# A two-layer hybrid decoder trunk: six of a layer's nine transposed projection blocks computed by rows, their queries and keys turned by VectorE, and work of GpSimd and VectorE moved to ScalarE

## The chip, the cores and the metric

The kernel runs on one core of one Trainium2 chip. The metric is device microseconds of one execution. Three executions of the kernel before gave 931.69, 933.27 and 933.47 us, a median of 933.27 us. The profiled execution, from which all rows below come, took 931.93 us by itself, with a span of 930.2 us from its first to its last instruction.

## The reference: what is computed

One sequence of 256 tokens goes through two layers of width 2048. A layer is a pre-norm mixer: one wide input projection (7700 columns) feeds four groups of four heads each, every group's output is multiplied by a gate path, and one output projection is added to the residual.

```python
def hybrid_layer(x, layer_idx, norm_g, w_in, ..., w_out, rope_diff, rope_moba):
    h = rms_norm(x, norm_g)
    p = split_columns(jnp.einsum("bsd,de->bse", h, w_in))
    log_f = jax.nn.log_sigmoid(p["fox_f"] + fox_fb)            # fox: softmax with a cumulative forget bias
    fox = forgetting_attention(q, k, v, log_f)                 # logit = q.k/sqrt(d) + F[t] - F[s]
    fox = from_heads(fox) * jax.nn.silu(p["fox_g"])
    q1, q2, k1, k2 = (partial_rope(t, *rope_diff) for t in (q1, q2, k1, k2))
    diff = differential_attention(q1, q2, k1, k2, v, lam)      # softmax(q1 k1) - lam softmax(q2 k2)
    diff = from_heads(rms_norm(diff, diff_norm_g) * (1.0 - lambda_init)) * jax.nn.silu(p["diff_g"])
    mq, mk = partial_rope(moba_q, *rope_moba), partial_rope(moba_k, *rope_moba)
    moba = from_heads(moba_attention(mq, mk, v)) * jax.nn.silu(p["moba_g"])
    gla = gla_chunked(q, k, v, log_a)                          # gated linear attention
    gla = from_heads(rms_norm(gla, gla_norm_g)) * jax.nn.silu(p["gla_g"])
    mixed = jnp.concatenate([fox, diff, moba, gla], axis=-1)
    return x + jnp.einsum("bse,ed->bsd", mixed, w_out)
```

The rotation of `partial_rope` touches a quarter of each head: 16 of 64 elements for diff, 32 of 128 for moba. After the second layer stands one more RMSNorm.

## The kernel before

**Products in three parts.** Weights and activations are 32-bit. Each is split into a high part that TensorE takes in its fp32r form and a low part with the rest; a product is hi·hi + lo·hi + hi·lo. ScalarE makes the high part of the weights (`hi`, line L185 in the trace is the helper that all VectorE and ScalarE calls go through), VectorE subtracts it (`lo<-raw,hi`).

**Steps.** The weights come in 304 steps of about 512 KB, 152 in each layer, in the order of a table made by `_steps` (steps 0 to 151 are layer 0, 152 to 303 layer 1). A step is one slice of one block; a block is a set of output columns (512 mostly) over all 2048 inputs. `load` sends a step's weights from the SP queue into one of 4 `raw` buffers. `parts_of` makes hi and lo in one of 4 `hi` and 4 `lo` buffers. `multiply` issues the matmuls. The Python loop at the end writes the program: in iteration i it first prepares step i+3 (hi and lo), then `settle` hands on the results of finished blocks, then step i is multiplied, then `tick` advances the background tasks (all the attention work, as generators). Every engine runs its instructions strictly in the order in which this loop wrote them, so a task's VectorE operation written in iteration i stands behind the `lo` of step i+3. That `lo` waits for a `hi`, and the `hi` of step i+3 waits until TensorE has read the `hi` of step i-1, which had the same buffer.

**Two kinds of block.** A block of kind "rows" has the activations as the stationary operand and 512 columns of weights moving: 12 matmuls of 512 columns a step (2 of the 16 input tiles, 2 halves of the tokens, 3 parts). A block of kind "cols" comes in two half-blocks of 256 columns, has the weights as the stationary operand, and gives the result transposed: 8 matmuls of 512 columns (both activation parts side by side in `hTp`) and 8 of 256 columns a step of 4 input tiles. A layer has nine such transposed blocks: gla_q with gla_k, fox_q, fox_k, fox_g, diff_q, diff_k, moba_q, moba_k, moba_g. Their result leaves PSUM by `columns` or `rotated`: a ScalarE copy (`both<-mm`), a VectorE addition (`both<-mm,both`), and a VectorE product, per half-block; for diff and moba also a shuffle on VectorE and a product on GpSimd for the rotation.

**PSUM.** Blocks accumulate in two `mm` buffers in turn, so a block can begin when the block before the last has been read out. The tasks' products go to two `side` buffers.

**Results that must wait.** `settle` holds a finished block back while a key that it needs is not ready (for moba_q the rotation table `rope_m`, which the task `turning` loads and scales by the row norms `rb`). When two finished blocks wait at the start of a new one, `settle` advances all tasks without limit (`tick(False)`) until the keys are there. In the same way the loop advances all tasks before a step of the output projection whose group of inputs (`mTh`, `mTl`, four groups) isn't ready yet. Otherwise `tick` stops when VectorE or ScalarE would get more work than TensorE's matmuls leave time for, by the estimates in `Costed`; the tasks that stand later in the list are then not advanced.

**Output projection.** Its blocks take the groups in the order gla, fox, diff, moba; the first two blocks are interleaved so that the moba inputs are asked for late. In the table of before the two blocks run over gla, fox and diff one after the other (6 steps each) and then over moba (2 steps each).

Of the kernel before, what the change touches and what calls it, by code (L numbers as in the profile page):

```python
# [21 lines left out]
P = 128  # L22
# [4 lines left out]
H = 4  # L27
# [11 lines left out]
T4 = 8  # L39
# [23 lines left out]
def _constants():  # L63
# [10 lines left out]
    put("after", (i[:, None] > i[None, :]))  # L74
    put("heads", np.stack([i < 64, i >= 64], 1))
    put("upto", (i[:, None] <= i[None, :]), "b")
# [6 lines left out]
    for name, half, dim in (("rope_d", DIFF_HALF, 64), ("rope_m", MOBA_HALF, HD)):  # L83
# [3 lines left out]
        cos, sin = np.ones((dim, SEQ), np.float32), np.zeros((dim, SEQ), np.float32)  # L87
        cos[:half] = cos[half:rot] = np.cos(ang)
        sin[:half], sin[half:rot] = -np.sin(ang), np.sin(ang)
        put(name, np.tile(np.concatenate([cos, sin], 1), (P // dim, 1)))  # L90
# [4 lines left out]
KEPT = CAT["rope_d"][0]  # L95


def _blocks():
# [37 lines left out]
def _steps():  # L136
# [78 lines left out]
def hybrid_trunk(  # L215
# [8 lines left out]
    diff_norm_g: bass.AP,  # L224
    gla_wa2: bass.AP,
    gla_ba: bass.AP,
    gla_norm_g: bass.AP,
# [59 lines left out]
    def turned(dst, src):  # L287


        for j in range(4):  # L290
            for i in range(4):
                a, b = slice(32 * i, 32 * i + 32), slice(32 * j, 32 * j + 32)
                v_.us += 0.14
                v_.transpose(dst[(b,) + (slice(None),) * (len(dst.shape) - 2) + (a,)],
                             src[(a,) + (slice(None),) * (len(src.shape) - 2) + (b,)])
            yield

# [10 lines left out]
    after = cst("after")  # L308
# [3 lines left out]
    dng = cp.tile([P, DEPTH, HD], F32, name="dng")  # L312
    gng = cp.tile([P, DEPTH, HD], F32, name="gng")
    wa = cp.tile([17, DEPTH, 256], F32, name="wa")
    upto_r = cp.tile([P, P], F32R, name="upto_r")
# [9 lines left out]
    nc.vector.memset(halfpow, -0.5)  # L325
    nc.vector.memset(one, 1.0)

    zeros = s4.get([P, 512], BF16)
    nc.vector.memset(zeros, 0.0)

# [10 lines left out]
    def constants():  # L341
# [5 lines left out]
        s = []  # L347
        for name in ("upto", "masks"):
            c, n = CAT[name]
            s.append(s4.get([P, n], BF16))  # L350
            nc.scalar.dma_start(s[-1], const_b[:, c:c + n])
# [357 lines left out]
    def softmax_part(m, qT, kT, rows, scale, su, forget=None):  # L709
# [3 lines left out]
        for kt in range(m + 1):  # L713
            dst = S[:, kt]
            if forget is not None:
                forget(dst, m, kt)
# [181 lines left out]
    def fox_k(l, ps, half):  # L898
# [4 lines left out]
        if half == 0:  # L903
            return
# [503 lines left out]
```

## Time and profile before

| | us |
|---|---|
| median of three executions | 933.27 |
| the profiled execution | 931.93 |
| its span | 930.2 |
| TensorE busy (matmul) | 918.1 |
| VectorE busy | 739.7 |
| ScalarE busy | 469.7 |
| GpSimd busy | 70.4 |

The span is what the instructions cover; the execution's own time is 1.7 us more. Matmuls are pipelined, so their durations overlap: what one costs in a row of equals is the distance between starts, not its own duration. A timeline row merges equal instructions that follow one another: start, time covered, engine, line, operation, tiles, count; in brackets how long the engine was idle before, and what released it. In the names of tiles buffer numbers are left out: `mm` and `side` are PSUM, `four` and `two` are work buffers of 4 KB and 2 KB per partition.

### The profile page before, as it was taken

The numbers are of one execution on the slowest core, as the hardware profiler recorded it, in microseconds if no ns is written. First come the engines' busy times: TensorE is split into PE (matmuls) and PEld (weight loads), VectorE is DVE, ScalarE is ACT, GpSimd is POOL, SyncE is SP. The second block draws the span as 40 slices with busy tenths as digits, with TensorE's granted clock in tenths as the row PEclk, the third lists the DMA queues.
The fourth block names the chain that finished last, engine by engine and source line by source line (L and its number), as shares of the span: only waits on it lengthen the run. The fifth ranks groups of instructions, "written<-read, shape, count | busy, mean of one in ns | idle before, by whom it ended". The sixth has DMA issues, their size and how long they took to land.

```text
span 930.2 us, 13911 instructions
## 1 busy us (share of the span) xinstructions
PE 918.1 (99%) x5302; PEld 803.1 (86%) x5302; DVE 739.7 (80%) x1181; ACT 469.7 (50%) x646; POOL 70.4 (8%) x45
## 2 busy tenths in 40 slices
PE   9999999999999999999999999999999999999996
PEld 7989889889888798888898898898888888888886
DVE  7668887899769979959856878777985898898663
ACT  7665634453474346444646553456446544463541
POOL 0011201001111100000000302000111101100000
PEclk9999999999999999999999999999999999999998
DMA  8766565555545565565654554554455546656452
GB/s 297 233 196 205 202 187 166 159 180 180 184 161 168 162 223 178 191 178 178 206 175 151 178 181 154 175 182 157 160 181 191 183 153 211 214 193 202 161 180 91
DMA packets 48645, 169.90 MB, mean 183 GB/s; under 512 B 5921, under 2 KB 6465, under 8 KB 48578
## 3 DMA queue, kind: packets, MB, share of 16 engines
q1 hardware_dynamic: 46304, 164.98, 54.4%
q10 hardware_dynamic: 1634, 1.93, 0.8%
q0 software_dynamic: 640, 2.10, 0.8%
q8 instruction: 41, 0.67, 0.3%
q14 instruction: 26, 0.21, 0.1%
HBM read 166.89 MB, written 2.10 MB: 182 GB/s over the span
## 4 chain that ended last, share of the span: by engine, by line
PE 94%; DVE 2%; DMA 1%; issue 1%; ACT 0%; SPq 0%; POOLq 0%; POOL 0%; DVEq 0%; ACTq 0%
PE mm L281 86%; PE side L281 8%; DVE lo L185 1%; DMA four<-in_xt 1%; DMA raw<-in_weights 1%; DVE four L185 0%; DVE tq L185 0%; PE side L285 0%; ACT hi L185 0%; DVE hTp L185 0%; DVE xs L185 0%; SPq L1185 0%; POOLq L1404 0%; POOL rf L392 0%; DVE both L185 0%
## 5 line engine op out<-in xcount | busy, mean ns | idle before, releaser
L185 ACT ACTIVATE hi<-raw 128x1024 fp32r<-128x1024 f32 (+3 forms) x301 | 317.5, 1059 | 402.9 <-PE mm L281 317.2
L185 DVE TENSOR_TENSOR lo<-raw,hi 128x1024 fp32r<-128x1024 f32 (+3 forms) x301 | 381.0, 1274 | 148.4 <-ACT hi L185 145.2
L281 PE MATMUL mm<-hTp,hi 128*128 128x512 f32 x1120 | 274.3, 393 | 0.0
L281 PEld LDWEIGHTS mm<-hTp,hi 128*128 128x128 f32 x1120 | 204.0, 188 | 39.7 <-issue 0.3
L281 PE MATMUL mm<-hi,hTp 128*128 128x512 f32 (+2 forms) x1024 | 196.3, 339 | 0.3 <-ACT hi L185 0.3
L281 PEld LDWEIGHTS mm<-hi,hTp 128*128 128x128 f32 x1024 | 161.0, 189 | 21.9 <-issue 0.7
L281 PEld LDWEIGHTS mm<-hTp,lo 128*128 128x128 f32 x1120 | 144.1, 191 | 5.5
L281 PE MATMUL mm<-hTp,lo 128*128 128x256 f32 x1120 | 147.3, 283 | 0.0
L281 PE MATMUL mm<-lo,hTp 128*128 128x512 f32 (+2 forms) x512 | 105.5, 338 | 0.2
L281 PEld LDWEIGHTS mm<-lo,hTp 128*128 128x128 f32 x512 | 80.9, 188 | 12.1 <-DVE lo L185 2.5
L185 DVE STREAM_TRANSPOSE four<-four 32x256 f32<-32x256 f32 x160 | 69.7, 435 | 2.5
L281 PE MATMUL mm<-hi,mTh 128*128 128x512 f32 (+1 forms) x256 | 64.6, 377 | 0.0
L281 PE MATMUL mm<-lo,mTh 128*128 128x512 f32 (+1 forms) x256 | 64.4, 376 | 0.0
L281 PE MATMUL mm<-hi,mTl 128*128 128x512 f32 (+1 forms) x256 | 64.4, 376 | 0.0
L281 PEld LDWEIGHTS mm<-lo,mTh 128*128 128x128 f32 x256 | 46.2, 188 | 8.8
L281 PEld LDWEIGHTS mm<-hi,mTl 128*128 128x128 f32 x256 | 46.2, 188 | 8.7
L281 PEld LDWEIGHTS mm<-hi,mTh 128*128 128x128 f32 x256 | 46.0, 188 | 8.6
L943 POOL TENSOR_TENSOR four<-four,two 128x1024 f32<-128x1024 f32 x8 | 21.4, 2669 | 277.2 <-DVE four L185 277.2
L281 PE MATMUL side<-four,four 128*128 128x128 f32 (+1 forms) x320 | 37.3, 276 | 0.0
L281 PEld LDWEIGHTS side<-four,four 128*128 128x128 f32 (+1 forms) x320 | 34.3, 190 | 2.2 <-issue 1.4
L185 ACT ACT_TABLE_LOAD x24 | 30.8, 1283 | 1.9 <-DVE an L185 1.5
L185 DVE TENSOR_TENSOR both<-mm,both 128x512 f32<-128x512 f32 x35 | 23.9, 683 | 0.0
(155 smaller groups left out, 629.1 us busy)
## 6 DMA issues: line engine op xcount, KB each, us to landing
raw<-in_weights SPq DMA_DIRECT2D x272, 512.0 KB, 3.6
raw<-in_weights SPq DMA_DIRECT2D x16, 516.0 KB, 3.6
raw<-in_weights SPq DMA_DIRECT2D x15, 528.0 KB, 4.3
xs<-in_x SPq DMA_DIRECT2D x4, 512.0 KB, 4.5
four<-in_xt SPq DMA_DIRECT2D x3, 512.0 KB, 6.3
out<-xs SPq DMA_DIRECT2D x4, 320.0 KB, 3.0
two<-in_const POOLq DMA_DIRECT2D x4, 256.0 KB, 3.0
two<-in_final_norm_g POOLq DMA_DIRECT2D x4, 256.0 KB, 5.7
```

Source lines behind the costliest of these rows:

```text
L185: return f(*args, **kw)
L281: t_.matmul(out, lhsT, rhs, start=start, stop=stop)
L943: g_.tensor_mul(sw, sw, over(f[:, 1], H))
```

## The change

Six of the nine transposed blocks of a layer (gla_q with gla_k, fox_q, fox_k, fox_g, diff_q, diff_k) become blocks of kind "rows"; the three of moba stay. Their results leave PSUM by two ScalarE operations with the row norm as scale (`rows_of`, or Silu for a gate). Where the transpose is needed, VectorE turns 32x32 blocks in 16 instructions (`turned`). The rotation of diff is done on rows, on the 16 rotating elements of each head alone. The fox output is made by rows, normalised and gated like diff and gla, and turned at the end. Turning an attention map leaves out the blocks above the diagonal, which GpSimd clears.

To ScalarE go: the scaling of the attention maps, the row scaling before the gate, the forget factors (from GpSimd), the diagonal of the gla map (from GpSimd), and the two largest of gla's seven copies under a mask. The norm weights of diff and gla are folded into the split of the result instead of a GpSimd product with the gate. Four matmuls a layer are dropped from the gla diagonal (it is now summed by VectorE from the rows), and the forget bias needs 6 instead of 8 wide matmuls a layer. At the start x comes in after every fourth step instead of every third, and the small `norm_gt` load goes from the SP queue to ScalarE's. In the output projection the first two blocks ask for diff later: 4 steps each over gla and fox, 2 each over diff, 2 each over moba.

```diff
@@ _blocks
-            ("cols", COL["gla_q"], 512),
+            ("rows", COL["gla_q"], 512),
...
-            ("cols", COL["fox_q"], 512),
-            ("cols", COL["fox_k"], 512),
+            ("rows", COL["fox_q"], 512),
+            ("rows", COL["fox_k"], 512),
...
-            ("cols", COL["fox_g"], 512),
-            ("cols", COL["diff_q"], 512),
-            ("cols", COL["diff_k"], 512),
+            ("rows", COL["fox_g"], 512),
+            ("rows", COL["diff_q"], 512),
+            ("rows", COL["diff_k"], 512),
@@ _steps
-                key = (9, i - b["c0"] // 512, j >= 12, i)
+                key = (9, i - b["c0"] // 512, max(j // 4, 1), i)
@@ new: how such a block is handed on
+    def by_rows(name, half=None, then=None):
...
+        def turn(l, t):
+            yield
+            if half:
+                yield from rotate(t)
+            z = yield from s4.take([P, H, SEQ])
+            yield from turned(z.rearrange("p h (m t) -> p m h t", m=2), t.rearrange("p m (h d) -> p m h d", h=H))
+            s4.put(t)
+            env[name, l] = z
+            ready.add((name, l))
+
+        def done(l, ps):
+            t = s4.get([P, 2, GW])
+            rows_of(l, ps, t, "a")
+            tasks.append(turn(l, t))
@@ gla
-        g_.tensor_mul(own, qkT[:, 0:2], qkT[:, 2:4])
-        yield
-        dg = yield from take_side()
-        for m in range(2):
-            for pair in range(2):
-                c = (m * 2 + pair) * 2
-                matmul(dg[:, c:c + 2], own[:, pair, m * P:(m + 1) * P], heads, True, True)
...
-        g_.tensor_mul(sT.rearrange("p m h t -> p (m h) t"), ident[:, None, :].to_broadcast([P, 8, P]),
-                      dgs[:, :, None].to_broadcast([P, 8, P]))
+        for c in range(8):
+            a_.activation(sT[:, c // 4, c % 4], ident, AF.Copy, scale=dgs[:, c:c + 1])
@@ normalised
-        v_.tensor_mul(p0, p0, rs[:, 0, :, None].to_broadcast([P, H, P]))
+        for h in range(H):
+            a_.activation(p0[:, h], p0[:, h], AF.Copy, scale=rs[:, 0, h:h + 1])
@@ gated_rows
-                v_.scalar_tensor_tensor(mixed[:, m, c], o[:, m, h], rs[:, m, h:h + 1], sg[:, m, c], op0=OP.mult, op1=OP.mult)
+                a_.activation(mixed[:, m, h * P:(h + 1) * P], o[:, m, h], AF.Copy, scale=rs[:, m, h:h + 1])
+            yield
+        side.put(ops)
+        v_.tensor_mul(mixed, mixed, sg)
@@ Forget
-                matmul(dst, upto_r, fg[0][:, m], True, False)
-                matmul(dst, upto_r, fg[1][:, m], False, False)
...
+            matmul(dst, ones_r, self.fg[0][:, kt], True, False)
+            matmul(dst, ones_r, self.fg[1][:, kt], False, False)
@@ dones
-            preceded(partial(turning, "rope_d"), gate_columns("fox_g")),
-            rotated("diff_q", "rope_d", DIFF_HALF, False),
-            started(diff, rotated("diff_k", "rope_d", DIFF_HALF, True)),
-            preceded(partial(turning, "rope_m"), diff_gate),
+            gate_rows("fox_g"), by_rows("diff_q", DIFF_HALF), by_rows("diff_k", DIFF_HALF, diff),
+            preceded(partial(turning, "rope_m"), gate_rows("diff_g")),
@@ load, prepare
-        if chunk == 0:
-            nc.sync.dma_start(ngt, norm_gt)
...
-        if i < 12 and i % 3 == 0:
-            load_x(i // 3)
+        if i < 16 and i % 4 == 0:
+            load_x(i // 4)
...
+            nc.scalar.dma_start(ngt, norm_gt)
```

Where the code moves instructions, the order of the built programs shows it. In what follows a number behind a tile's name is only its place in the program; a larger one was written later.

VectorE, layer 1, around moba_q, before. `lo_6606` is step 233, `lo_6629` to `lo_6770` are steps 234 to 239; `side1_6596` are diff's first logits, `two4_6682` the moba rotation table, `mm_6661` the first half-block of moba_q (steps 232 to 235):

```order
L185 TENSOR_TENSOR lo_6606<-raw_6525,hi_6605 128x1024
L185 TENSOR_TENSOR side1_6596<-side1_6596,neg_b_88 128x1024
L185 TENSOR_REDUCE mx8_6624<-side1_6596 128x8
L185 TENSOR_SCALAR nb8_6626<-mx8_6624 128x8
L185 TENSOR_TENSOR lo_6629<-raw_6543,hi_6628 128x1024
...
L185 TENSOR_TENSOR two4_6682<-two4_6682,rb_4536 128x512
L185 TENSOR_TENSOR lo_6730<-raw_6632,hi_6729 128x1024
L185 TENSOR_TENSOR lo_6770<-raw_6655,hi_6769 128x1024
L185 TENSOR_TENSOR both_6777<-mm_6661,both_6777 128x512
```

The same place in the changed program. `lo_6600` is step 243, `lo_6654` step 244; `side1_6609` are diff's first logits, `two0_6605` the rotation table, `mm_6405` and `mm_6507` the two half-blocks of moba_q (steps 232 to 235 and 236 to 239):

```order
L189 TENSOR_TENSOR lo_6600<-raw_6505,hi_6599 128x1024
L189 TENSOR_TENSOR side1_6609<-side1_6609,neg_b_87 128x1024
L189 TENSOR_REDUCE mx8_6619<-side1_6609 128x8
L189 TENSOR_SCALAR nb8_6621<-mx8_6619 128x8
L189 TENSOR_TENSOR two0_6605<-two0_6605,rb_4419 128x512
L189 TENSOR_TENSOR both_6626<-mm_6405,both_6626 128x512
L189 STREAM_SHUFFLE four1_6625<-both_6626 128x512
L189 TENSOR_TENSOR four7_6624<-both_6626,two0_6605 128x512
L189 TENSOR_TENSOR both_6631<-mm_6507,both_6631 128x512
L189 STREAM_SHUFFLE four1_6625<-both_6631 128x512
L189 TENSOR_TENSOR four7_6624<-both_6631,two0_6605 128x512
L189 TENSOR_TENSOR lo_6654<-raw_6529,hi_6653 128x1024
```

The read-out of moba_q's first half-block stood behind the `lo` of step 239 and now stands behind that of step 243, with the logits' three operations and the table's product ahead of it, and both half-blocks are read out between the same two `lo`.

TensorE at that place in the changed program; `hi_6501` is step 239 and `hi_6525` step 240, which begins moba_k in the buffer of `mm_6405`:

```order
L285 MATMUL mm_6507<-hTp_111,lo_6502 128x256 x8
L285 MATMUL mm_6507<-hTp_111,hi_6501 128x512 x8
L285 MATMUL side1_6609<-four0_6346,four5_6074 128x128 x8
L285 MATMUL mm_6636<-hTp_111,hi_6525 128x512 x8
L285 MATMUL mm_6636<-hTp_111,lo_6526 128x256 x8
```

The product of diff's first logits, which stood in the stretch of the diff gate, stands between moba_q and moba_k.

VectorE, layer 1, the first blocks of the output projection, before; `lo_7959` is step 286, and `mTl_114` is the low part of the moba group, first read in step 284:

```order
L185 TENSOR_TENSOR lo_7920<-raw_7829,hi_7919 128x1024
L185 TENSOR_TENSOR four5_7937<-side0_7906,gate1_7410 128x1024
L185 TENSOR_TENSOR lo_7940<-raw_7851,hi_7939 128x1024
L185 TENSOR_TENSOR lo_7959<-raw_7874,hi_7958 128x1024
L185 TENSOR_TENSOR mTl_114<-four5_7937,mTh_113 128x1024
L185 TENSOR_TENSOR lo_7978<-raw_7892,hi_7977 128x1024
```

The same place in the changed program, where `lo_7752` is step 286 and `lo_7771` step 287; the moba group is again first read in step 284:

```order
L189 TENSOR_TENSOR lo_7732<-raw_7642,hi_7731 128x1024
L189 TENSOR_TENSOR four2_7749<-side1_7718,gate1_7184 128x1024
L189 TENSOR_TENSOR lo_7752<-raw_7664,hi_7751 128x1024
L189 TENSOR_TENSOR lo_7771<-raw_7686,hi_7770 128x1024
L189 TENSOR_TENSOR mTl_113<-four2_7749,mTh_112 128x1024
L189 TENSOR_TENSOR lo_7790<-raw_7704,hi_7789 128x1024
```

The low part of the moba group has moved back by one `lo`, from behind step 286 to behind step 287.

## Rows read from the trace of the kernel before

**Rows 1.** The page: engines' busy time (share of the span, instructions), the final chain

```profile
PE 918.1 (99%) x5302; PEld 803.1 (86%) x5302; DVE 739.7 (80%) x1181; ACT 469.7 (50%) x646; POOL 70.4 (8%) x45
...
PE 94%; DVE 2%; DMA 1%; issue 1%; ACT 0%; SPq 0%; POOLq 0%; POOL 0%; DVEq 0%; ACTq 0%
```

**Rows 2.** Timeline of TensorE: two pairs of transposed steps, two steps by rows

```profile
172.63 3.82 PE L281 MATMUL mm<-hTp,hi 128*128 128x512 f32 x16
...
178.20 3.82 PE L281 MATMUL mm<-hTp,hi 128*128 128x512 f32 x16
...
235.53 1.98 PE L281 MATMUL mm<-hi,hTp 128*128 128x512 f32 x8
...
238.25 1.98 PE L281 MATMUL mm<-hi,hTp 128*128 128x512 f32 x8
```

**Rows 3.** Groups by line, shapes apart, TensorE: count, busy us, mean ns, idle before

```profile
L281 PE MATMUL side<-ct,two 128*128 128x2 f32 x16 | 1.9, 243 | 0.0
```

**Rows 4.** Timeline, first 60 us, TensorE

```profile
1.25 4.45 PE L334 MATMUL side<-four 128*128 128x512 bf16 x10 [1.25 <-DVE four L329]
...
5.23 2.18 PE L281 MATMUL mm<-hi,hTp 128*128 128x264 f32 x8
...
8.22 1.24 PE L281 MATMUL mm<-hi,hTp 128*128 128x264 f32 x8 [0.32 <-ACT hi L185]
...
30.74 0.80 PE L281 MATMUL side<-one,four 128*128 128x1 f32 x6 [0.67 <-DVE four L185]
```

**Rows 5.** Timelines of TensorE and VectorE around gla's second product in layer 0

```profile
120.39 2.00 PE L281 MATMUL mm<-hTp,hi 128*128 128x512 f32 x8
...
123.95 1.83 PE L281 MATMUL side<-tq,eight 128*128 128x128 f32 x14 [1.56 <-DVE eight L185]
...
122.28 0.68 DVE L185 TENSOR_TENSOR both<-mm,both 128x512 f32<-128x512 f32 x1
123.00 0.69 DVE L185 TENSOR_TENSOR four<-both,rb 128x512 f32<-128x512 f32 x1
```

**Rows 6.** Timelines of TensorE and ScalarE: diff's product, hand-over of a hi buffer, two late steps

```profile
249.22 1.16 PE L281 MATMUL side<-four,four 64*128 64x128 f32 x16
...
302.64 1.98 PE L281 MATMUL mm<-hi,hTp 128*128 128x512 f32 x8
...
302.84 1.06 ACT L185 ACTIVATE hi<-raw 128x1024 fp32r<-128x1024 f32 x1 [2.69 <-PE mm L281]
...
319.10 1.98 PE L281 MATMUL mm<-hi,hTp 128*128 128x512 f32 x8
...
322.18 2.00 PE L281 MATMUL mm<-hi,hTp 128*128 128x512 f32 x8
```

**Rows 7.** Groups by line, shapes apart, VectorE and ScalarE

```profile
L185 DVE TENSOR_TENSOR lo<-raw,hi 128x1024 fp32r<-128x1024 f32 x268 | 339.8, 1277 | 123.6 <-ACT hi L185 120.4
...
L185 DVE STREAM_TRANSPOSE four<-four 32x256 f32<-32x256 f32 x160 | 69.7, 435 | 2.5
...
L185 DVE TENSOR_TENSOR mTl<-four,mTh 128x1024 fp32r<-128x1024 f32 x8 | 9.7, 1219 | 0.0
...
L185 DVE TENSOR_TENSOR two<-two,rb 128x512 f32<-128x512 f32 x4 | 2.7, 686 | 0.0
...
L185 DVE TENSOR_TENSOR side<-side,neg_b 128x1024 f32<-128x1024 f32 x2 | 2.5, 1225 | 0.0
...
L185 DVE TENSOR_REDUCE mx<-side 128x8 f32<-128x1024 f32 x2 | 2.5, 1225 | 0.1
...
L185 DVE TENSOR_SCALAR nb<-mx 128x8 f32<-128x8 f32 x2 | 0.3, 171 | 0.1
...
L185 ACT ACTIVATE hi<-raw 128x1024 fp32r<-128x1024 f32 x268 | 282.9, 1060 | 360.0 <-PE mm L281 280.4 <-DMA raw<-in_weights 37.2 <-issue 23.0
```

**Rows 8.** Windows at the end: length, busy us (count) of PE, PEld, DVE, ACT, POOL, PEclk, DMA share, GB/s

```profile
920.00:925.00 5.00, 2.30 (x20) 2.10 (x18) 1.63 (x5) 1.17 (x3) 0.67 (x1) 1.00 0.55 210
...
925.00:930.20 5.20, 0.00 (x0) 0.00 (x0) 0.36 (x1) 0.28 (x1) 0.00 (x0) 0.54 0.53 202
```

More of the change, by code (lines that the diff above doesn't have):

```diff
@@ L307, in hybrid_trunk @@
     ident = cst("ident")
-    after = cst("after")
+    since = [cst("after"), cst("upto")]
     heads = cst("heads")
@@ L563, in gla_first, with gla_qk, gla_turn @@
         tasks.append(gla(l, an))
-    def gla_qk(l, ps, half):
-        rb = over(env["rb", l], 2)
-        if half == 0:
-            env["gla_qk", l] = s4.get([P, 4, SEQ])
-            v_.scalar_tensor_tensor(env["gla_qk", l][:, 0:2], summed(ps), 0.125, rb, op0=OP.mult, op1=OP.mult)
-        else:
-            v_.tensor_mul(env["gla_qk", l][:, 2:4], summed(ps), rb)
-            ready.add(("gla_qk", l))
+    def gla_qk(l, ps):
+        t = s4.get([P, 2, GW])
+        rows_of(l, ps, t, "a")
+        tasks.append(gla_turn(l, t))
+    def gla_turn(l, t):
+        yield
+        own = yield from s2.take([P, 2, H, 64])
+        q, k = (t[:, :, i * 256:(i + 1) * 256].rearrange("p m (h d) -> p m h d", h=H) for i in range(2))
+        for m in range(2):
+            v_.tensor_mul(own[:, m], q[:, m], k[:, m])
+        dgs = sm.tile([P, 2, H], F32, name="dgs", bufs=2)
+        v_.tensor_reduce(dgs, own, axis=AX.X, op=OP.add)
+        s2.put(own)
+        env["dgs", l] = dgs
+        yield
+        z = yield from s4.take([P, 4, SEQ])
+        yield from turned(z.rearrange("p c (m t) -> p m c t", m=2), t.rearrange("p m (c f) -> p m c f", c=4))
+        s4.put(t)
+        env["gla_qk", l] = z
+        ready.add(("gla_qk", l))
     def gla_gate(l, ps):
@@ L884, in fox_forget @@
             for m in range(2):
-                g_.tensor_mul(z[:, m], after[:, None, :].to_broadcast([P, H, P]), pf[:, m, :, None].to_broadcast([P, H, P]))
+                for h in range(H):
+                    a_.activation(z[:, m, h], since[m], AF.Copy, scale=pf[:, m, h:h + 1])
             forget.fg.append(z)
-            y = yield from s2.take([P, H, P], F32R)
-            v_.tensor_copy(y, pf[:, 1, :, None].to_broadcast([P, H, P]))
-            forget.f1.append(y)
             yield
         ready.add(("forget", l))
-    def fox_q(l, ps, half):
-        if half == 0:
-            env["fox_q", l] = s4.get([P, H, SEQ])
-        columns(l, ps, env["fox_q", l], half)
@@ L898, in fox_k, with fox @@
-    def fox_k(l, ps, half):
-        if half == 0:
-            env["fox_k", l] = s4.get([P, H, SEQ])
-        kT = env["fox_k", l]
-        columns(l, ps, kT, half)
-        if half == 0:
-            return
-        def run():
-            yield from until(("forget", l))
-            yield
-            yield from attend_columns(l, 0, "fox", env["fox_q", l], kT, env["forget", l])
-        tasks.append(run())
+    def fox(l):
+        yield from until(("fox_q", l))
+        yield from until(("fox_k", l))
+        yield from until(("forget", l))
+        yield
+        yield from attend_rows(l, 0, "fox", env["fox_q", l], env["fox_k", l], env["forget", l])
@@ L914, in turning, with gate_rows, done @@
+    def gate_rows(name):
+        def done(l, ps):
+            sg = sgs.get([P, 2, GW])
+            r = env["r", l]
+            for m in range(2):
+                a_.activation(sg[:, m], ps[m], AF.Silu, scale=r[:, m:m + 1])
+            env[name, l] = sg
+            ready.add((name, l))
+        return done
     def turning(name, l):
@@ L1168, in hybrid_trunk @@
             l, f = next(dones)
[L1169 removed]
+        own = {COL["moba_q"]: ("rope_m",)}.get(z["c0"] if z["w"] == "w_in" else None, ())
         blocks.append({"kind": z["kind"], "lhs": hT if z["w"] == "w_in" else mT, "n": z["n"], "per": z["per"],
@@ L1330, in prepare @@
     def prepare(i):
-        if 0 < i < 12 and i % 3 == 0:
-            split_xt([i // 3 * 4 + k for k in range(4)])
+        if 0 < i < 16 and i % 4 == 0:
+            split_xt([i + k for k in range(4)])
         if i < len(plan):
```

223 lines of the change are left out of this document (130 added, 93 removed).

## The prediction

> **What bounds the kernel now.** I read the page first: TensorE is busy for 918.1 of 930.2 us, and 94% of the chain that ended last is TensorE; VectorE has 80%, ScalarE 50%, GpSimd 8% [rows 1]. So the time is the sum of TensorE's instructions and of the few places where it stands still. For the sum I read the timeline of TensorE for the distance between the starts of equal steps, since busy durations overlap. Two transposed steps lie between 172.63 and 178.20, so one takes 2.783 us; two starts by rows, 235.53 and 238.25, are 2.720 apart [rows 2]. For the idle places I went through TensorE's rows for brackets, and through the steps whose distance is over the usual one.
>
> Hardly anything else counts by its sum. VectorE counts by its order: an operation written behind a `lo` can't run before that `lo`, and that `lo` can't before TensorE lets go of a `hi` buffer (the `lo` group's idle time, 123.6 us, is ended for 120.4 by a `hi`, and the `hi` group's for 280.4 by a matmul [rows 7]). So I followed VectorE's order at every place where TensorE needs something other than `lo`.
>
> **The change part by part: TensorE's own work.** Six blocks of 8 steps in two layers, 96 steps, go from 2.783 to 2.720 us: 96 × 0.063 = 6.1 us less. They are the same columns, but 12 matmuls instead of 16 a step. The gla diagonal loses its 16 small matmuls, 1.9 us busy [rows 3]. The forget bias loses two wide matmuls a layer, each recorded twice in the trace: 4 × 0.227 (2.720 / 12 [rows 2]) = 0.9 us. Together 8.9.
>
> The Trainium skill, "TensorE: Matmul & The Clock Gate", section "Wait — 56ns, not 53.3ns?", gives N ÷ 2.4 GHz plus about 2.5 ns for a matmul of N columns in a row of such. By that a step of either kind has 2.56 us of columns, and the four matmuls fewer are worth 0.01 us a step, 1.0 us in all instead of 6.1. The rows above differ by 0.063 a step, so the trace doesn't agree here, and the row decides; its outcome is near the fourth rival below.
>
> **Old waits that go.** (a) At the start TensorE waits 0.32 for a `hi` and 0.67 for `four` before the sums of squares [rows 4]. The small load leaves the SP queue, so the second halves of the weights behind it are sent earlier, and x comes every fourth step, so that product has more room: 1.0 less. (b) At 122.4 TensorE waits 1.56 us for VectorE's masked copies of gla; just ahead of these stood two read-outs of fox, 0.68 and 0.69 [rows 5]. These become ScalarE's: 0.68 + 0.69 = 1.4 less. (c) Late steps by rows in the fox and diff stretch: 319.10 to 322.18 is 3.08 instead of 2.72 [rows 6]. There are four of these, at 319 to 325 and at the same place of the other layer, behind VectorE's normalising and gating, part of which goes to ScalarE: 4 × 0.36 = 1.4 less. Together 3.8, and with the work 12.7.
>
> **New waits.** The changed order puts three things behind a later `lo`. Let T be the end of the last step before each place.
>
> First, layer 0, step 88, the start of moba_k, which needs the buffer of moba_q's first half. Its read-out stands behind the logits' three operations, the table's product and the `lo` of step 90. Back from T lie steps 87 and 86 (2 × 2.783) and diff's product of 1.1 (16 records at 249.22 [rows 6]), so `hi` 89 can begin at T − 6.7 + 0.2; 0.2 is the hand-over from 302.64 to 302.84 [rows 6]. With `hi` 1.06 and `lo` 1.28 the `lo` of 89 ends at T − 4.1; then 1.23 + 1.23 + 0.17 + 0.69 (logits, maximum, its negative, table [rows 7]) end at T − 0.8, `lo` 90 at T + 0.5, and the read-out of 0.68 [rows 5] at T + 1.2. TensorE waits 1.2 us.
>
> Second and largest, layer 1, step 240, the start of moba_k there. Both halves of moba_q are still held back, and the tasks are driven on by force until the table is ready. On VectorE this puts `lo` 243 first, whose `hi` needs the buffer of step 239, that is T: 0.2 + 1.06 + 1.28, then 1.23 + 1.23 + 0.17 + 0.69, then the read-out, 0.68: T + 6.5. TensorE has only diff's product, 1.1, in between. It waits 5.4 us. The work that hides such a read-out elsewhere, three prepared steps, stands behind it here and hides nothing. Who waits for it: only moba_k and what follows, but that is the whole of TensorE.
>
> Third, layer 1, step 284, the first use of moba's inputs: `mTl` stands behind `lo` 287 now. `hi` 287's buffer comes free 0.7 before T (steps end with hi·`mTl`, so the last use of `hi` is late); with the hand-over, 1.06 and 1.28 `lo` ends near T + 1.7 and `mTl` (1.22 [rows 7]) at T + 2.9. TensorE has four matmuls without it, 0.9: it waits 2.0 us. Together 8.6.
>
> **The clock after the 5.4 us.** No wait of before is as long. At the start ten equal matmuls take 4.45 us and those at 5.23 still twice what those at 8.22 take [rows 4]: TensorE runs at 1.2 GHz for its first 6 us or so and at 2.4 GHz from about 7.2. At the end the granted clock is 1.00 up to 925 and 0.54 over the rest, with the last matmul near 922.3 [rows 8]; a fall somewhere near 925.4 gives that mean. After the 1.56 us at 122 matmuls keep their pace [rows 5]. So 5.4 us of idling is nearer to the idling that ended in a fall (about 3.1 us) than to that which did not. The bounds are 0 (no fall) and 3.0 (six microseconds at half pace); I take 2.0. The same page of the Trainium skill, section "Part 1: The HAM clock gate (the "warmup" mystery)", says "the default state is throttled, and activity releases the throttle"; the start and the end of this trace agree, and no row of before shows it in the middle.
>
> **What lies beside other work.** VectorE gains 156 transposes of 256 columns net at 0.435 [rows 7], 68 us, and loses read-outs, rotations, scalings and copies; counted by kinds of instruction at the rows' durations it goes from 741 to 755, still 160 under TensorE. ScalarE goes from 470 to about 514. GpSimd loses 43 of 70 us and gets 36 clearings of small blocks. None of it is TensorE's, and each step by rows asks for `hi` and `lo` at the same pace as a transposed one, so I cost all of it at nothing; the cover is the lead of three steps, some 8.2 us, that `lo` has. What it costs where that lead is used up is the third rival.
>
> **The sum.** 931.9 (profiled execution) − 12.7 + 8.6 + 2.0 = 929.8. The profiled execution is 1.3 below the median of 933.27; I add half of that, since I can't tell how the runs of the changed kernel will lie: 930.5, or 0.3% less than 933.27.
>
> **Rivals.** 1. The clock stays up over the 5.4 us, as after 1.56: 928.5. For it: the only fall is at the very end, without any work behind it. 2. The new waits don't come, because the order that I priced by hand has slack that I don't see (ScalarE or VectorE earlier by a few us there): 930.5 − 8.6 − 2.0 = 919.9, or some 922 with the small ones left. Against it: `hi` 243 can't be earlier than T by its buffer. 3. **Slower:** VectorE becomes the bound in gla's stretch. In steps 40 to 47 of layer 0 twelve more transposes, and in 192 to 199 of layer 1 sixteen, are written between the `lo`. That is 28 × 0.435 = 12.2 us, less four read-outs of 1.37 [rows 5], 5.5: 6.7 us more there, and all of it is TensorE's if VectorE has no idle time left in that stretch: 930.5 + 6.7 = 937.2. It decides from the point where VectorE's work between one `lo` and the `lo` three steps later is over the lead of 8.2 us. Against it: before, `lo` had 123.6 us of waiting to give away [rows 7]. 4. The steps by rows are no faster, if the 0.063 belongs to the stretch and not to the kind, since the columns are the same: 930.5 + 6.1 = 936.6. (By the rule above from the Trainium skill's page "TensorE: Matmul & The Clock Gate" 1.0 of it would stay, 935.6.) Against it: both distances were taken where nothing waits, and the steps of the output projection, also of 512 columns, keep 0.227 a matmul. 5. The change doesn't do what it says for the old waits; they come back at the next late thing: 930.5 + 3.8 = 934.3.
>
> **How the numbers follow.** The forecast with its two values of the clock has 65% (48 and 17 for the first rival), no new waits 10, VectorE bound 8, steps by rows not faster 7, old waits stay 10. The forecast's own range is 927.5 to 933, from the clock's bounds (2.0 down, 1.0 up) and a microsecond either way for the hand counts. The range that holds 8 in 10 leaves out the slower rival, most of the fourth and some of the one without new waits: 924.5 to 935.7. A measurement of this kernel can tell about 0.2% from no change, that is 1.9 us: below 931.4 is faster, above 935.1 slower. Of the forecast proper 930.5 lies close to that edge, so some 27 of its 48 fall on the faster side and 21 on the same; of the first rival 14 and 3; the one without new waits 10 faster; old waits stay 8 same, 2 slower; the fourth 3 same, 4 slower; VectorE 8 slower. Faster 0.51, same 0.35, slower 0.14.
>
> **What would show it.** In the profile of after: steps by rows 2.72 apart in the stretches of gla_q, fox and diff (2.78 would be rival 4); no wait near 122, at the two places of the start, or at 319 to 325; TensorE idle for about 5.4 us at the start of moba_k in layer 1, released by VectorE's read-out, and 1.2 at the same place in layer 0; about 2.0 idle in the first blocks of the output projection of layer 1, released by `mTl`; matmuls at 0.45 us for some microseconds after the long one, and a granted clock below 1. Wrong would make it: steps late by VectorE throughout gla's stretch, or a shorter wait at step 240.

## The result and the profile after

The changed kernel takes 938.73 us (median of five, 937.16 to 939.54), the kernel before beside it 932.36 (931.69 to 933.47). The ratio is 1.0064, with a 95% interval of 1.005 to 1.0078: slower by 0.6%, where 0.3% faster was forecast. The profiled execution took 939.54 us with a span of 937.7, 7.5 us more than the span before.

The page's first part: busy time of each engine, share of the span, instructions; and the clock granted to TensorE in 40 slices.

```profile
PE 914.2 (97%) x4898; PEld 785.5 (84%) x4898; DVE 738.2 (79%) x1248; ACT 505.5 (54%) x780; POOL 37.7 (4%) x59
...
PEclk9999999999999999999999999999999899999998
```

Beside [rows 1]: TensorE has 3.9 us less of busy time in a span that is 7.5 us longer. VectorE is where it was, ScalarE has 36 us more, GpSimd 33 less. So no engine took over; the time is in TensorE's idling. What TensorE waited for, summed by releaser (total us, times, longest; L189 and L285 are in the changed kernel the helpers that L185 and L281 were before):

```profile
PE mm L285 <- DVE both L189: 5.8, 2, 5.2
PE side L285 <- DVE eight L189: 3.2, 2, 2.3
PE mm L285 <- DVE hTp L189: 2.3, 1, 2.3
PE mm L285 <- DVE mTl L189: 1.8, 1, 1.8
PE side L347 <- DVE halfpow L341: 1.2, 1, 1.2
PE side L289 <- DVE an L189: 0.9, 1, 0.9
PE side L285 <- DVE four L189: 0.5, 1, 0.5
```

The first line is the read-out of moba_q before moba_k in both layers (5.20 and 0.55), the fourth `mTl`: both were forecast. The second is gla's product, whose old wait [rows 5] should have gone; the third is the start; the fifth, at the very start, was there before too (1.25 [rows 4]); the sixth and seventh I had not looked for.

Added up from the distances between TensorE's starts, its matmuls at their usual spacing come to 910.1 us before and 902.4 now, 7.7 less. What lies over the usual spacing (waits and slow matmuls) went from 10.9 to 26.2, some 15 more. The difference is the 7.5 us of the spans.

The long wait, in VectorE's timeline of layer 1 (start, time covered, engine, line, operation, tiles, count; idle time before, and its releaser):

```profile
731.62 1.23 DVE L189 TENSOR_TENSOR lo<-raw,hi 128x1024 fp32r<-128x1024 f32 x1 [1.21 <-ACT hi L189]
732.77 1.22 DVE L189 TENSOR_TENSOR side<-side,neg_b 128x1024 f32<-128x1024 f32 x1
734.02 1.22 DVE L189 TENSOR_REDUCE mx<-side 128x8 f32<-128x1024 f32 x1
735.28 0.17 DVE L189 TENSOR_SCALAR nb<-mx 128x8 f32<-128x8 f32 x1
735.36 0.68 DVE L189 TENSOR_TENSOR two<-two,rb 128x512 f32<-128x512 f32 x1
735.97 0.68 DVE L189 TENSOR_TENSOR both<-mm,both 128x512 f32<-128x512 f32 x1
```

and in TensorE's:

```profile
730.43 1.16 PE L285 MATMUL side<-four,four 64*128 64x128 f32 x16
736.79 3.75 PE L285 MATMUL mm<-hTp,hi 128*128 128x512 f32 x8 [5.20 <-DVE both L189]
740.34 2.50 PE L285 MATMUL mm<-hTp,lo 128*128 128x256 f32 x16
```

It is the prediction's list, one operation after the other, 5.20 us against 5.4. The eight matmuls behind it take 3.55 us up to the next start instead of 1.8, and the next 16 take 2.34 instead of 1.9: 2.1 us, against 2.0 forecast. But there are two more such places. In the granted clock (windows: length, busy us and count of PE, PEld, DVE, ACT, POOL, then PEclk, DMA share, GB/s):

```profile
103.00:107.00 4.00, 4.00 (x15) 3.34 (x15) 3.86 (x10) 1.61 (x5) 0.00 (x0) 0.57 0.59 222
736.80:743.00 6.20, 6.20 (x26) 5.42 (x27) 4.18 (x7) 1.06 (x1) 2.57 (x1) 0.64 0.00 0
873.00:879.00 6.00, 5.89 (x19) 4.70 (x20) 1.28 (x2) 1.32 (x2) 0.00 (x0) 0.72 0.39 115
8.00:10.00 2.00, 2.00 (x11) 2.00 (x10) 2.00 (x5) 1.31 (x2) 0.00 (x0) 0.50 1.04 424
```

The first stretch stands behind an idling of 2.31 us, the third behind one of 1.78. Each costs about 1.7 us in the distances between starts. The last stretch is at the start of the kernel: there the clock had already risen (1.00 from 4.1 to 7.4) and was at 0.50 again behind the idling of 2.3 us. In the table below that is part of the start.

Around 99 us, first VectorE's timeline:

```profile
94.02 2.38 DVE L189 TENSOR_TENSOR tq<-eight,four 64x128 f32<-64x128 f32 x8
96.43 1.23 DVE L189 TENSOR_TENSOR lo<-raw,hi 128x1024 fp32r<-128x1024 f32 x1
97.57 0.22 DVE L189 SCALAR_TENSOR_TENSOR fx<-mm,rstd,fb 128x4 f32<-128x4 f32 x1
98.39 0.22 DVE L189 SCALAR_TENSOR_TENSOR fx<-mm,rstd,fb 128x4 f32<-128x4 f32 x1 [0.60 <-ACT four L189]
98.53 1.78 DVE L189 TENSOR_TENSOR tq<-eight,four 64x128 f32<-64x128 f32 x6
100.34 1.23 DVE L189 TENSOR_TENSOR lo<-raw,hi 128x1024 fp32r<-128x1024 f32 x1
101.48 1.51 DVE L189 TENSOR_TENSOR eight<-eight,four 128x128 f32<-128x128 f32 x7
```

then ScalarE's:

```profile
97.89 0.47 ACT L189 ACTIVATE four<-mm,rstd 128x254 f32<-128x254 f32 x1 [4.08 <-DVE fx L189]
```

and TensorE's:

```profile
98.44 1.07 PE L285 MATMUL mm<-lo,hTp 128*128 128x512 f32 x4
101.82 2.29 PE L285 MATMUL side<-tq,eight 128*128 128x128 f32 x14 [2.31 <-DVE eight L189]
```

VectorE works almost without a pause from 94.02 on, and gla's products stand between three `lo`. ScalarE meanwhile stood 4.08 us for the small `fx`, which left late because of them, and the next `hi` with it. Which of the two is the cause can't be told from these rows.

### The profile page after: what moved, and what is told of

Read it like the earlier page. It is cut to its first block, busy times and chain, and to the rows that moved or that the text cites. A ratio compares the mean times of both kernels' runs of the same rounds, so it can differ in the third digit from the quotient of the medians.

```text
span 937.7 us, 13284 instructions
## 1 busy us (share of the span) xinstructions
PE 914.2 (97%) x4898; PEld 785.5 (84%) x4898; DVE 738.2 (79%) x1248; ACT 505.5 (54%) x780; POOL 37.7 (4%) x59
## 5 line engine op out<-in xcount | busy, mean ns | idle before, releaser
L189 ACT ACTIVATE hi<-raw 128x1024 fp32r<-128x1024 f32 (+3 forms) x301 | 316.6, 1059 | 337.8 <-PE mm L285 264.4
L189 DVE TENSOR_TENSOR lo<-raw,hi 128x1024 fp32r<-128x1024 f32 (+3 forms) x301 | 372.4, 1244 | 152.3 <-ACT hi L189 148.1
L285 PE MATMUL mm<-hi,hTp 128*128 128x512 f32 (+2 forms) x1728 | 381.0, 365 | 2.3 <-DVE hTp L189 2.3
L285 PEld LDWEIGHTS mm<-hi,hTp 128*128 128x128 f32 x1728 | 296.4, 190 | 52.6 <-ACT hi L189 3.1
L285 PE MATMUL mm<-lo,hTp 128*128 128x512 f32 (+2 forms) x864 | 203.4, 362 | 0.0
L285 PEld LDWEIGHTS mm<-lo,hTp 128*128 128x128 f32 x864 | 149.6, 189 | 25.1
L189 DVE STREAM_TRANSPOSE four<-four 32x256 f32<-32x256 f32 (+1 forms) x352 | 148.6, 422 | 5.7
L285 PE MATMUL mm<-hTp,hi 128*128 128x512 f32 x384 | 95.3, 397 | 5.8 <-DVE both L189 5.8
L285 PEld LDWEIGHTS mm<-hTp,hi 128*128 128x128 f32 x384 | 71.3, 191 | 20.2 <-issue 5.4
L285 PE MATMUL mm<-hi,mTl 128*128 128x512 f32 (+1 forms) x256 | 64.8, 378 | 1.8 <-DVE mTl L189 1.8
L285 PE MATMUL mm<-hi,mTh 128*128 128x512 f32 (+1 forms) x256 | 65.5, 381 | 0.0
L285 PE MATMUL mm<-lo,mTh 128*128 128x512 f32 (+1 forms) x256 | 65.0, 378 | 0.0
L285 PEld LDWEIGHTS mm<-hi,mTl 128*128 128x128 f32 x256 | 46.4, 190 | 11.1 <-DVE mTl L189 2.2
L285 PEld LDWEIGHTS mm<-hi,mTh 128*128 128x128 f32 x256 | 46.6, 191 | 8.8
L285 PEld LDWEIGHTS mm<-lo,mTh 128*128 128x128 f32 x256 | 46.4, 189 | 8.8
L285 PEld LDWEIGHTS mm<-hTp,lo 128*128 128x128 f32 x384 | 49.9, 193 | 2.0
L285 PE MATMUL mm<-hTp,lo 128*128 128x256 f32 x384 | 50.7, 285 | 0.0
L285 PE MATMUL side<-four,four 128*128 128x128 f32 (+1 forms) x320 | 36.5, 277 | 0.5 <-DVE four L189 0.5
L285 PEld LDWEIGHTS side<-four,four 128*128 128x128 f32 (+1 forms) x320 | 33.8, 190 | 3.2 <-issue 1.4
L189 ACT ACTIVATE four<-mm,rstd 128x512 f32<-128x512 f32 (+2 forms) x36 | 21.1, 632 | 6.2 <-DVE fx L189 6.2
L189 ACT ACTIVATE four<-side,nb 128x256 f32<-128x256 f32 (+1 forms) x48 | 20.4, 436 | 5.1 <-DVE nb L189 5.1
```

The source lines that it names most:

```text
L189: return f(*args, **kw)
L285: t_.matmul(out, lhsT, rhs, start=start, stop=stop)
```

## The experiments

The theory after the result: TensorE's work fell about as forecast, and the loss is a handful of single waits, each with its place in VectorE's order, and the clock behind the longer ones (A). The rival: VectorE has become the bound in the stretches where work was added, and a wait taken away comes back at the next place (B). All ratios are to the kernel before, measured beside it; the changed kernel has 1.0064.

**The start and the first block.** Loads and order of the first 50 us:

```diff
+        if chunk == 0:
+            nc.sync.dma_start(ngt, norm_gt)
-            nc.scalar.dma_start(ngt, norm_gt)
...
         for m in range(2):
             v_.tensor_scalar(an[:, m], ...)
+        for m in range(2):
             a_.activation(sg[:, m, :248], ps[m][:, 16:], AF.Silu, scale=r[:, m:m + 1])
```

> The changed kernel with two places of its first 50 us put back or reordered: the small load norm_gt goes first on the SP queue again, and in the reading of the first block both VectorE products for the gate factors (an) stand ahead of ScalarE's two Silu. Theory A (the time is lost in single waits, each with its own place): the first matmul on weights starts near 5.2 us instead of 7.24, as before the change, if the weights' first half is late only because of the loads beside it, or near 6.9 if that half (ready for ScalarE at 6.29) is late by itself; the idle 0.85 before the second transposition of an near 50 us goes. Together 1 to 3 us less than the changed kernel, about 936.5. Theory B (VectorE bounds the early stretch, waits only move): the same idle time returns within the first 100 us, and the time stays near 938.7.

Measured: 934.75 us, ratio 1.0034 (1.0021 to 1.0046). The first matmul on weights starts at 5.98 instead of 7.24, behind ScalarE's `hi`, and `an` is gone from the list of waits. TensorE's and ScalarE's rows:

```profile
5.98 1.47 PE L285 MATMUL mm<-hi,hTp 128*128 128x264 f32 x8 [0.36 <-ACT hi L189]
...
5.22 0.64 ACT L189 ACTIVATE hi<-raw 128x528 fp32r<-128x528 f32 x1 [2.99 <-DMA raw<-in_weights]
```

The wait of 2.3 us at gla's product is still there, but in this execution the clock stayed up behind it. So the two places were worth 1.3 and 0.9 us between these two executions, as A has it; the rest of the 2.8 us between the ratios may be the clock. The start is not quite the old one: 5.98 against 5.23 [rows 4]. The first half of the weights is still late, ready for ScalarE at 5.22 instead of 3.72, though the small load is back on the SP queue. The start also varies: in the changed kernel and the four experiments that share its start, TensorE idled there for 2.3, 0.8, 0.9, 1.7 and 0.9 us, and the first matmul on weights came at 7.24, 6.45, 6.53, 6.64 and 6.57. In the three profiled kernels with the load put back it came at 5.98, 5.91 and 6.04. So the moved load is worth 0.4 to 0.7 us, and the changed kernel's own profiled execution was an unlucky one.

**The rotation table at the head of the tasks.**

```diff
             if half != 1:
-                tasks.append(task(l))
+                tasks.insert(0, task(l))
```

> The changed kernel, with the task that makes moba's rotation table put at the head of the list of tasks instead of its end. On VectorE the table's product is then written before moba_q's results are held back, and the two read-outs stand behind the lo of steps written before moba_k. Theory A: in layer 1 the 5.4 us before step 240 go, and the eight slow matmuls behind them (1.6 us at 1.2 GHz); in layer 0 the 0.7 at moba_k. At step 284 the gate product and mTl both stand behind the lo of step 287 now, so the 1.9 us there grow to about 4. Sum: 938.7 - 5.4 - 1.6 - 0.7 + 2.3 = about 933.3. Theory B (the table's product was not what the wait hung on): no change of the 5.4 us, 938.7.

Measured: 935.68 us, ratio 1.004 (1.0026 to 1.0055). TensorE's waits in this kernel:

```profile
PE mm L285 <- DVE mTl L189: 3.3, 1, 3.3
PE side L285 <- DVE eight L189: 3.2, 2, 2.3
PE mm L285 <- ACT mTh L189: 2.4, 1, 2.4
```

Both waits for `both` are gone, the 5.20 and the 0.55, so the table's product was what they hung on. But most of it is given back. The other tasks are later: diff's `mTl` now comes 3.3 us late, which I had not foreseen, and moba's `mTh` 2.4, which I had (4 in all were expected there), each with slow matmuls behind it. My reading is that the forced advance had also pushed diff's work ahead; no run shows that by itself.

**ScalarE ahead of VectorE at the first block of fox.**

```diff
         for m in range(2):
-            v_.scalar_tensor_tensor(fx[:, m], ...)
             a_.activation(vn[:, m, 258:], ps[m][:, :254], AF.Copy, scale=r[:, m:m + 1])
+        for m in range(2):
+            v_.scalar_tensor_tensor(fx[:, m], ...)
```

> The changed kernel with one swap where the first block of fox leaves PSUM: ScalarE's two copies ahead of VectorE's two small products (fx) instead of in turn. In the changed kernel ScalarE stood 4.08 us for fx at 93.8 to 97.9, which stood behind six to eight products of gla on VectorE; so the next hi came at 99.02, its lo ended at 101.6, gla's seven products behind it, and TensorE waited 2.31 us. Theory A: with the swap hi comes some 4 us earlier, and the wait of 2.31 us near 99.5 and the six slow matmuls behind it (1.3 us) go: about 935.1. Theory B (VectorE's own work is what is late there): ScalarE's wait goes, TensorE's stays at 1 us or more, 937 to 938.7.

Measured: 934.76 us, ratio 1.0028 (1.0019 to 1.0038), which looks like A's number. The rows say B. ScalarE's timeline:

```profile
92.12 0.81 ACT L189 ACTIVATE four<-mm,rstd 128x254 f32<-128x254 f32 x2
92.82 1.05 ACT L189 ACTIVATE hi<-raw 128x1024 fp32r<-128x1024 f32 x1
```

and TensorE's:

```profile
99.54 1.83 PE L285 MATMUL side<-tq,eight 128*128 128x128 f32 x14 [1.64 <-DVE eight L189]
```

ScalarE no longer waits and `hi` is 4.6 us earlier, against TensorE's steps, yet TensorE still idles 1.64 of the 2.31 us: VectorE's own products and `lo` fill the time. That the total fell by more is the clock, which stayed up behind 1.64 us in this execution, and a shorter start. So `fx` was 0.7 us of the cause, and VectorE's queue the rest.

**The long wait filled.**

```diff
+        if i == 240:
+            warm = side.get([P, 1024])
+            for _ in range(24):
+                t_.matmul(warm[:, :512], ones_r, hTp[:, 0].rearrange("p z t -> p (z t)"), start=True, stop=True)
+            side.put(warm)
         multiply(s)
```

> The changed kernel with 24 matmuls of 512 columns (24 x 0.227 = 5.4 us) written before step 240 of layer 1, where TensorE stood idle; their result is used by nobody. VectorE's order is unchanged. Theory A (the slow matmuls behind the wait are the price of the idling itself): the granted clock stays at 2.4 GHz there, the eight matmuls of 0.427 us become 0.227, and the time falls by about 1.6 us, to 937.1, with not one wait removed. Theory B (the clock falls there for another reason, or the matmuls delay the read-out): the slow matmuls stay, 938.7 or a little more.

Measured: 934.61 us, ratio 1.0028 (1.0016 to 1.004). TensorE's timeline around step 240:

```profile
729.61 5.84 PE L1439 MATMUL side<-hTp,ones_r 128*128 128x512 f32 x24
735.28 1.98 PE L285 MATMUL mm<-hTp,hi 128*128 128x512 f32 x8
737.10 1.11 PE L285 MATMUL mm<-hTp,lo 128*128 128x256 f32 x8
```

and the granted clock there (1.00 behind the busy times):

```profile
735.00:741.00 6.00, 6.00 (x35) 5.26 (x35) 5.68 (x7) 1.06 (x1) 2.58 (x1) 1.00 0.01 3
```

The eight matmuls take 1.82 us again, the clock is at 2.4 GHz: the slow ones behind the wait are the price of the idling, as A says, and they go without one wait removed. The fall in the total is larger than the 1.6 expected; in this execution the clock also stayed up behind the waits of 2.3 and 1.8 us elsewhere; the first of those lies ahead of the filled place, so the filling can't be why. It is not the profiled execution alone: the mean granted clock was 0.995 to 0.998 in the six executions of this kernel and 0.988 to 0.991 in the five of the changed one. Why the falls elsewhere were rarer here, the runs don't show.

**One yield more in gla.**

```diff
             v_.tensor_mul(ee[:, 1, NL], ee[:, 1, NL], qv[:, 1])
+            yield
             for m in range(2):
                 pcs = yield from take_side()
```

> The changed kernel with one more yield in gla, so that TensorE's first product of tq and eight is written one step of weights (2.72 us) later and VectorE's products stay where they are. Theory A (the two waits near 99 and 137 are VectorE's queue being longer than the lead, 2.31 and 0.86 us): one step more covers both; minus 3.4 us with their small change, and the slow matmuls behind the first. A side effect can be read from the order: later tasks shift a step, and at step 240 of layer 1 the logits' three operations stand ahead of the lo of step 243 instead of behind it; only that lo and the read-out are left behind T, 0.2 + 1.06 + 1.28 + 0.68 = 3.2 us of idling instead of 5.4. Sum about 938.7 - 3.4 - 2.2 - 1.3 = 931.8. Theory B (VectorE is the bound over the whole gla stretch): the wait returns a step later with 1 us or more, about 936.

Measured: 929.43 us, ratio 0.9971 (0.996 to 0.9981): one line makes the changed kernel faster than the one before. TensorE at the two places:

```profile
98.54 1.98 PE L285 MATMUL mm<-hi,hTp 128*128 128x512 f32 x8
100.36 1.07 PE L285 MATMUL mm<-lo,hTp 128*128 128x512 f32 x4
101.26 1.72 PE L285 MATMUL side<-tq,eight 128*128 128x128 f32 x14
...
728.98 2.88 PE L285 MATMUL mm<-hTp,hi 128*128 128x512 f32 x8 [3.10 <-DVE both L189]
```

Gla's product starts without a wait, at the next step of weights, and doesn't wait later either, so VectorE isn't the bound of the stretch; its queue there was only longer than the lead, the time that the order leaves between VectorE's operation and TensorE's use of it. At step 240 3.10 us are left, where 3.2 was read from the order. Of the 10.3 us between the two profiled executions (939.54 and 929.23) the two waits at gla are 3.2, the shorter one at step 240 is 2.1, and the start, which the line doesn't touch, 1.4. The remaining 3.6 are mostly the clock, at gla and behind `mTl`, where it stayed up without any change to the 1.8 us of waiting.

**All of them.** `ngt` and `an` as in the first, the yield in gla, the table's task first, and no yield between the two halves of the split where no norm weight is folded in (moba, and by the same line fox):

```diff
         hi_of(mT[0][:, kts], src, 1.0 if g is None else g)
-        yield
+        if g is not None:
+            yield
```

> The changed kernel with every wait taken away that its profile shows after the start: norm_gt first on the SP queue, an ahead of Silu, one yield more in gla, the task of moba's rotation table at the head of the list, and no yield between the two parts of the moba group's split, so that mTl stands behind the lo of step 286. The arithmetic is the same. Theory A (the change saves 8.9 us of TensorE's work and the time was lost in single waits and in the clock behind them): TensorE idles for less than 2 us after the first 10 us; the changed kernel's 939.5 of the profiled execution less 2.3 + 0.4 + 0.7 + 1.0 + 2.5 + 1.3 + 1.0 + 0.7 + 5.4 + 1.6 + 1.9 + 1.3, where the start's 2.3 may stay by half: 920 to 922, faster than before by 1.1%. Theory B (a wait removed comes back elsewhere): 928 or more.

Measured: 919.14 us (919.11 to 919.32), ratio 0.9863 (0.9849 to 0.9876), 1.4% faster than before and 2.0% faster than the changed kernel. TensorE's waits, the whole list:

```profile
PE side L347 <- DVE halfpow L341: 1.2, 1, 1.2
PE side L285 <- DVE four L189: 0.5, 1, 0.5
PE mm L285 <- ACT hi L189: 0.5, 1, 0.5
```

and its clock on the page:

```profile
PEclk9999999999999999999999999999999999999999
```

A holds: nothing came back. VectorE has 737.3 us of work in it, as much as in the kernel that lost time. The waits of 3.3 and 2.4 us that the table's task brought when it was moved alone aren't there either; which of the other edits keeps them away, no run separates.

**The form alone.** The last kernel with the six blocks' weights stationary again, 8 matmuls of 512 columns with hi and 8 of 256 with lo:

```diff
+        if b["w"] == "w_in" and b["c0"] in WIDE:
+            for part in ("hi", "lo"):
+                for j, kt in order:
+                    for c in range(4):
+...
+            return
         if b["kind"] == "rows":
```

> The kernel without the waits, with the six blocks' matmuls issued in the transposed form again (weights stationary, 8 matmuls of 512 and 8 of 256 columns a step instead of 12 of 512), into the same PSUM; the sums that come out are not those of the blocks, everything else is issued as it was. This measures the price of the form alone. Theory A (my reading, 2.783 against 2.720 us a step): 96 x 0.063 = 6.1 us more than the kernel without the waits. Theory B (the columns alone set the pace): no difference, at most 1 us.

Measured: 925.17 us (925.02 to 925.21), ratio 0.9927 (0.9913 to 0.994): 925.17 − 919.14 = 6.03 us more, against 6.1 expected. Two steps of diff in this kernel, and two of the one above:

```profile
178.68 2.00 PE L285 MATMUL mm<-hTp,hi 128*128 128x512 f32 x8
...
184.27 2.00 PE L285 MATMUL mm<-hTp,hi 128*128 128x512 f32 x8
```

```profile
176.98 1.98 PE L285 MATMUL mm<-hi,hTp 128*128 128x512 f32 x8
...
182.42 1.98 PE L285 MATMUL mm<-hi,hTp 128*128 128x512 f32 x8
```

2.795 and 2.72 us a step. 96 times their difference would be 7.2 us, so the price is not the same at every step. The order isn't quite the old one either: this kernel changes between hi and lo twice in each step, where the kernel before runs 16 of a kind over two steps and takes 2.783 a step [rows 2]. So the run confirms the size to about a microsecond. The Trainium skill, "TensorE: Matmul & The Clock Gate", section "Wait — 56ns, not 53.3ns?", gives about 2.5 ns a matmul beyond its columns; by an estimate from that figure the 384 matmuls fewer are worth 1.0 us. The run doesn't agree, and the measurement decides.

**The kernel before with the same yield.** The line of the fifth experiment alone, in the kernel before.

> The kernel before with the one yield more in gla and nothing else: its wait of 1.56 us near 122 should go. Theory A (each of these waits is one place of the order and can be taken away alone): 1.6 us less than the kernel before, 930.1 where that is 931.7, and what is then left between it and the kernel without the waits is TensorE's work. Theory B (it comes back): 931.7.

Measured: 930.4 us, ratio 0.9982 (0.9974 to 0.9991), 1.6 us less, the number of A. The rows are less clear. The wait near 122 is gone, but the one for the sums of squares near 30 is 1.3 us in this execution and one of 1.0 us appears near 576; the listed waits, without the one at the very start, only fall from 2.8 to 2.3 us. So B is not excluded for the old kernel. It had less to win from this line: 1.6 us, against the 8.7 that the same line gave the changed one (1.0064 to 0.9971).

## Why the prediction was wrong, point by point

Each term for the profiled execution, in us, from the traces of the changed kernel and of [rows 1 to 8]; the clock is counted from the distances of the slow matmuls:

| step of the prediction | forecast | measured |
|---|---|---|
| six blocks by rows | −6.1 | −6.0 |
| small matmuls dropped | −2.8 | −2.5 |
| start | −0.3 | +1.9 |
| sums of squares at 30 | −0.7 | −0.7 |
| gla's product | −1.4 | +1.4 |
| late steps by rows | −1.4 | about −1.5 |
| moba_k, layer 0 | +1.2 | +0.6 |
| moba_k, layer 1 | +5.4 | +5.2 |
| `mTl`, layer 1 | +2.0 | +1.8 |
| `an`, and moba's product at 398 | none | +1.4 |
| slow clock | +2.0 | +5.5 |
| sum | −2.1 | +7.1 |

The measured sum is 0.4 to 0.5 below the real difference (7.5 in span, 7.6 in time); the terms were read one by one, and that much is their error. The slow clock of the start is in the start's term.

**What was right.** The work of the six blocks, to about a microsecond, by an experiment of its own; the small matmuls (the gla diagonal's 16 took 1.65 us from start to start, not 1.9, and the forget bias went from 3.90 to 3.02); and the three new waits, which were read from the order of VectorE by adding up the durations of [rows 6, 7]: 8.6 forecast, 7.6 measured. Of the slips in that working none matters: by the rows shown a transposed step is 2.785 us, not 2.783, and the third wait's terms add up to T + 1.8, not 1.7. VectorE's and ScalarE's work was put too high, 755 and 514 us against 738.2 and 505.5. The fourth rival (rows no faster) falls with the 6.03.

**What failed: "old waits that go".** I let the waits of [rows 4] and [rows 5] vanish because something that stood ahead of them was moved, and didn't count out what stands there now, as I had done for the new waits. At gla's product I took away two read-outs of 1.4 us and asked nothing more. In the changed order VectorE's products on gla meet the transposes and `fx`, the product of TensorE has moved with them, and 2.31 and 0.86 us are waited in place of 1.56 and 0.19. At the start I priced one load that leaves the SP queue, and not what ScalarE's queue holds then: the first half of the weights was ready for ScalarE at 6.29 instead of 3.72, and `ngt`, behind it, for VectorE at 6.75. That is 5.0 of the 9.2 us between the sums: 2.2 at the start, 2.8 at gla. Of the start's, 1 us or so is chance, and the moved load accounts for 0.4 to 0.7, by the executions named with the first experiment. The rest stays open, since the weights' half is late with the load put back too. One rival was not tested: the load of constants behind it on ScalarE's queue grew from 129 to 225 KB with the change, which the list of changes doesn't name.

**What failed: "the clock after the 5.4 us".** Its size was right, 2.1 against 2.0. I priced it at one of the three places where it fell, because 1.56 us of idling had not brought it down before: 3.5 us. One of the two others is a wait that I had forecast myself, the 2.0 us for `mTl`.

**What was not seen.** `an` stands behind ScalarE's Silu and its table load, 0.85, and moba's product in layer 0 behind transposes, 0.48: 1.4 with what follows them. I had looked for waits where the diff moved blocks, not where it moved the time at which they are wanted.

**The slower rival** had the right sign and the right stretch, and the wrong mechanism. VectorE bound over gla's 8 steps would have cost 6.7 and would not have gone with one yield. It was a queue longer than its lead at one point; that its number, 937.2, came near 938.73 is luck. The rival that I should have written is that the old waits come back larger.

## What to carry to other kernels

A wait is not removed by moving what stood in front of it. Count out what stands in front of it in the new order, with the same care as for a wait that the change adds, and do it for every product that TensorE takes from VectorE. And where engines run in written order, look first for the line that lets the consumer ask one step later: here one yield was worth 8.7 us between the ratios, more than the 6.0 that the new form of the six blocks saved. Of these only 3.2 are the two waits that it was written for; the rest is a shorter wait at another place, the clock, and chance at the start.

## What the runs showed of the hardware

**The clock fell behind some short waits, but not always.** Behind 5.2 us of idling it fell in all three profiled executions that had it, and behind 2.4, 3.1 and 3.3 in the one that had each. Behind the 2.3 at gla's product it fell in two (the changed kernel, the table's) and stayed up in two (the start's, the filled one); behind the 1.8 at `mTl` it fell in three (the changed kernel, the start's, fox's) and stayed in two (filled, one yield more). At the start, soon after its first rise, it fell behind 2.3 us in the changed kernel and behind 1.7 in the filled one. Behind 1.64 and less it fell in none. So a wait of 2 us here costs either 2 or 3.7, from one execution to the next, and the runs don't tell what decides. The Trainium skill's "TensorE: Matmul & The Clock Gate", section "Part 1: The HAM clock gate (the "warmup" mystery)", has it that the default state is throttled and that activity releases the throttle. The fourth experiment agrees as far as it goes: where TensorE was kept active with matmuls of no use, the granted clock stayed at 1.00, 2.4 GHz.

**Two matmuls of 256 columns take some 13 ns longer than one of 512 in this kernel.** One of 512 columns takes 0.227 us from start to start and one of 256 columns 0.120. Read as a fixed part of 13 ns a matmul, four matmuls fewer a step make 0.053 of the 0.063 us. It doesn't reach further down: those of 128 columns are 0.112 apart (14 in 1.72 at 101.26 in the fifth experiment), where the same sum would give 0.067.

**VectorE's products on 64 partitions are not cheaper.** `tq` (64x128) takes 0.30 us from start to start, eight in 2.38; `eight` (128x128, the same 128 elements a partition) 0.20, seven in 1.51. The fourteen `tq` ahead of gla's product would take 1.4 us less at 0.20. What makes the difference, the partitions or something else, no run shows.
